# One 512-column matmul for both activation parts, in 512-column weight blocks with rows taken by fours

## The chip, the core and the metric

The kernel runs on one NeuronCore of a Trainium2 chip. The metric is the device time of one execution in microseconds (us). TensorE (PE) multiplies into PSUM, VectorE (DVE) and ScalarE (ACT) do everything elementwise, and all loads are issued in order from SyncE's queue (SP).

## The reference, cut to what matters

Two layers work on a residual stream x of 256 tokens by 2048 features, in float32. Everything is a function of x, of one conditioning vector c, and of some 580 MB of weights that are read once.

```
for layer in range(2):
    mod = silu(c) @ ada_w[layer] + ada_b[layer]          # 2048 x 12288, a matrix by ONE vector
    sh1, sc1, g1, sh2, sc2, g2 = split(mod, 6)
    h = rmsnorm(x, norm_mix) * (1 + sc1) + sh1
    proj = h @ w_in[layer]                               # 2048 x 4608: qa ka va | qb kb vb
    mixed = concat(diff_attention(...), window_gqa_sink(...)) @ w_out[layer]     # 2048 x 2048
    x = x + g1 * mixed
    h2 = rmsnorm(x, norm_mlp) * (1 + sc2) + sh2
    x = x + g2 * (square(relu(h2 @ w_up[layer])) @ w_down[layer])   # 2048 x 8192, 8192 x 2048
return rmsnorm(x, final_norm)
```

## The kernel before, in words

Activations lie with the feature on the partition: a chunk is 128 features by 256 tokens. To keep float32 accuracy on TensorE, every weight row block and every activation is split into a high part (a cast to the fp32r type) and a low part (the rest), and a product is the sum of three matmuls: weight high by activation high, weight high by activation low, weight low by activation high (`mm3`, lines 359, 360, 361; line 387 for the first row block of a product, with the same three in another order). A call of `gemm` takes a block of 1024 weight columns over all its rows of 128: per row block one DMA of 512 KB brings `raw`, `split` makes `whi` on ScalarE (line 347) and `wlo` on VectorE (line 348), and `emit` runs 8 column tiles of 128 by 3 matmuls of 256 columns into four PSUM banks (`acc`), two column tiles to a bank. Values with tokens on the partition (va, vb) go the other way round: there the weights are the moving operand, 512 columns wide, by the same three lines.

The pools set how far the engines run ahead: 6 `raw` tiles, 8 tiles for `whi` and `wlo` (four row blocks), 4 `acc` banks, 48 slots `b` of [128, 2, 256] for activations and partial sums. The order on each engine is fixed when the program is built; each engine works through its own list in order.

The product of `ada_w` by the vector is not on TensorE: VectorE multiplies and adds it row by row (`ada`, line 199), fed by its own DMAs (`araw`) into the same `raw` pool. `feed(rate)` spreads these units between the row blocks of the other products, from the start to somewhat past the start of layer 1's MLP. So VectorE has three kinds of work beside TensorE: the `wlo` of each row block, the `ada` units, and what finishes a product: `residual` (line 706) for w_out and w_down, `settle` and `fin_up` for w_in and w_up, `hilo` (lines 450, 451) for the split of a new activation.

Stages in the trace by the first load of each weight: layer 0's w_in from 26 us, w_out 314, w_up (first half of the columns, in two K groups of 8 row blocks) 465, w_down (first half of the rows) 660, w_up second half 851, w_down second half 1042; layer 1's w_in 1229, w_out 1493, w_up 1618, w_down 1809, w_up 1993, w_down 2178 to about 2388.

## Time and profile before

| what | value |
|---|---|
| device time, median of 3 runs | 2404.28 us (2403.33 to 2410.04) |
| span of the profiled execution | 2402.5 us |
| PE busy | 2293.4 us, 17875 matmuls |
| VectorE busy | 1652.5 us |
| ScalarE busy | 1165.0 us |
| read from HBM | 581.66 MB, 243 GB/s over the span |

The span runs from the first to the last instruction of the profiled execution; the timed runs are 1.8 us above it at the median, which is what lies around the span. Matmul records overlap (one lasts 284 ns and the next starts 120 ns after it), so PE's busy share says only that its queue was not empty; the distance from one start to the next says what a matmul costs in a full stream.

### The profile page before, as it was taken

What the parts mean: (1) busy time and instruction counts of PE and PEld (TensorE: products, weight loads), DVE (VectorE), ACT (ScalarE), POOL (GpSimd) and SP (SyncE); (2) the same over time, 40 slices, a digit from 0 to 9 for tenths busy, and PEclk for the clock granted to TensorE, in tenths of its full rate; (3) what the DMA queues carried; (4) which work ended last, traced back from release to release, by engine and by line L of the source; (5) the groups of instructions that cost most, each with busy time, mean ns of one, the idle gap of its engine ahead of it and who ended that gap; (6) DMA issues with size and microseconds to landing.
All of it is one profiled execution on the core that took longest, in us unless ns stands there. A gap on an engine that the chain in (4) does not pass through costs nothing.

```text
span 2402.5 us, 44175 instructions
## 1 busy us (share of the span) xinstructions
PE 2293.4 (95%) x17875; PEld 2218.0 (92%) x17875; DVE 1652.5 (69%) x1995; ACT 1165.0 (48%) x1947; POOL 0.2 (0%) x4
## 2 busy tenths in 40 slices
PE   5888999899999999999989999999999999999998
PEld 3777898899999999999989898898999999999998
DVE  6799878887876667776768887888644444454453
ACT  4445664465433334644435557645554333454343
POOL 0000000000000000000000000000000000000000
PEclk8899999999999999999999999999999999999999
DMA  8998756898677888888886994586865555555552
GB/s 285 330 316 291 235 166 210 299 328 314 202 266 275 282 272 301 299 294 296 282 273 244 309 324 133 193 281 233 302 186 184 184 185 184 181 171 194 184 183 98
DMA packets 205776, 586.66 MB, mean 244 GB/s; under 512 B 22498, under 2 KB 31364, under 8 KB 205572
## 3 DMA queue, kind: packets, MB, share of 16 engines
q1 hardware_dynamic: 205572, 583.85, 72.3%
q8 instruction: 140, 2.29, 0.4%
q14 instruction: 64, 0.52, 0.1%
HBM read 581.66 MB, written 2.10 MB: 243 GB/s over the span
## 4 chain that ended last, share of the span: by engine, by line
PE 61%; DMA 3%; DVE 2%; ACT 2%; issue 1%; SPq 0%; DVEq 0%; ACTq 0%
PE acc L360 18%; PE acc L361 18%; PE acc L359 18%; PE acc L387 3%; DMA araw<-in_ada_w_dram 2%; DVE wlo L348 1%; PE misc L586 1%; PE lg L601 1%; PE misc L495 1%; PE misc L206 0%; ACT whi L347 0%; PE lg L648 0%; PE misc L578 0%; ACT tmp L459 0%; PE misc L518 0%
## 5 line engine op out<-in xcount | busy, mean ns | idle before, releaser
L359 PE MATMUL acc<-b,whi 128*128 128x256 f32 x5000 | 1417.7, 284 | 5.8 <-ACT whi L347 5.8
L360 PE MATMUL acc<-b,whi 128*128 128x256 f32 x5000 | 1415.1, 284 | 0.0
L361 PE MATMUL acc<-b,wlo 128*128 128x256 f32 x5000 | 1409.7, 284 | 5.6 <-DVE wlo L348 5.1
L347 ACT CAST whi<-raw 128x1024 fp32r<-128x1024 f32 (+1 forms) x726 | 743.7, 1032 | 1007.3 <-PE acc L360 771.4
L348 DVE TENSOR_TENSOR wlo<-raw,whi 128x1024 fp32r<-128x1024 f32 (+1 forms) x726 | 862.9, 1200 | 451.2 <-ACT whi L347 447.8
L359 PEld LDWEIGHTS acc<-b,whi 128*128 128x128 f32 x5000 | 960.4, 192 | 10.1 <-ACT whi L347 7.2
L361 PEld LDWEIGHTS acc<-b,wlo 128*128 128x128 f32 x5000 | 955.9, 192 | 12.0 <-DVE wlo L348 8.5
L360 PEld LDWEIGHTS acc<-b,whi 128*128 128x128 f32 x5000 | 960.9, 192 | 2.8 <-issue 2.0
L199 DVE SCALAR_TENSOR_TENSOR ada<-araw,c_act,ada 128x1024 f32<-128x1024 f32 (+1 forms) x375 | 464.9, 1240 | 160.4 <-DMA araw<-in_ada_w_dram 158.2
L387 PE MATMUL acc<-b,whi 128*128 128x256 f32 x720 | 149.7, 300 | 20.2 <-ACT b L559 8.4
L387 PEld LDWEIGHTS acc<-b,whi 128*128 128x128 f32 x720 | 123.3, 205 | 24.2 <-ACT b L559 9.4
L387 PE MATMUL acc<-b,wlo 128*128 128x256 f32 x360 | 94.7, 300 | 3.5 <-DVE wlo L348 3.5
L387 PEld LDWEIGHTS acc<-b,wlo 128*128 128x128 f32 x360 | 73.7, 208 | 4.4 <-DVE wlo L348 4.4
L451 DVE TENSOR_TENSOR b<-tmp,b 128x512 fp32r<-128x512 f32 x72 | 49.5, 689 | 32.2 <-ACT b L450 31.9
L706 DVE SCALAR_TENSOR_TENSOR x<-acc,mod,x 128x256 f32<-128x256 f32 x128 | 54.8, 479 | 21.4 <-PE acc L361 21.3
L360 PE MATMUL acc<-wlo,b 128*128 128x512 f32 (+1 forms) x152 | 56.5, 372 | 3.2 <-DVE wlo L348 3.2
L208 ACT ACTIVATE misc<-misc 128x128 f32<-128x128 f32 x192 | 50.2, 261 | 18.8 <-PE misc L206 17.7
L361 PE MATMUL acc<-whi,b 128*128 128x512 f32 (+1 forms) x152 | 55.9, 367 | 0.0
L450 ACT CAST b<-tmp 128x512 fp32r<-128x512 f32 x72 | 44.6, 619 | 21.9 <-DVE tmp L797 19.4
L359 PE MATMUL acc<-whi,b 128*128 128x512 f32 (+1 forms) x152 | 52.8, 372 | 2.3 <-ACT whi L347 2.1
L559 ACT ACTIVATE b<-tmp,mod 128x256 fp32r<-128x256 f32 x62 | 34.4, 596 | 9.1 <-DVE mod L218 5.1
L360 PEld LDWEIGHTS acc<-wlo,b 128*128 128x128 f32 x152 | 28.7, 189 | 9.7 <-DVE wlo L348 5.4
(171 smaller groups left out, 1230.7 us busy)
## 6 DMA issues: line engine op xcount, KB each, us to landing
araw<-in_ada_w_dram SPq DMA_DIRECT2D x512, 256.0 KB, 4.9
raw<-in_w_up_dram SPq DMA_DIRECT2D x256, 512.0 KB, 4.6
raw<-in_w_down_dram SPq DMA_DIRECT2D x256, 512.0 KB, 4.7
raw<-in_w_in_dram SPq DMA_DIRECT2D x144, 512.0 KB, 5.5
araw<-in_ada_w_dram SPq DMA_DIRECT2D x128, 512.0 KB, 5.5
raw<-in_w_out_dram SPq DMA_DIRECT2D x64, 512.0 KB, 5.4
b<-in_x_dram SPq DMA_DIRECT2D x8, 256.0 KB, 5.0
out_dram<-tmp SPq DMA_DIRECT2D x8, 256.0 KB, 2.7
```

Of the source, the lines that this page charges most:

```text
L199: nc.vector.scalar_tensor_tensor(acc, raw[:, j, :], cc, acc, op0=ALU.mult, op1=ALU.add)
L208: nc.scalar.activation(pm[:, t * P : (t + 1) * P], pm[:, t * P : (t + 1) * P], AF.Copy, accum_out=m[:, t0 + t : t0 + t + 1])
L347: nc.scalar.copy(hi, raw)
L348: nc.vector.tensor_tensor(lo, raw, hi.bitcast(F32), op=ALU.subtract)
L359: nc.tensor.matmul(o, lhsT=lhi, rhs=rhi, start=first, stop=False, skip_group_check=True)
L360: nc.tensor.matmul(o, lhsT=lhi, rhs=rlo, start=False, stop=False, skip_group_check=True)
L361: nc.tensor.matmul(o, lhsT=llo, rhs=rhi, start=False, stop=last, skip_group_check=True)
L387: nc.tensor.matmul(banks[t // 2][:, t % 2, :], lhsT=w1[:, t * P : (t + 1) * P], rhs=a2, start=a2 is ahi and w1 is hi and t % 2 == 0, stop= ...
L450: nc.scalar.copy(hi, src)
L451: nc.vector.tensor_tensor(lo, src, hi.bitcast(F32), op=ALU.subtract)
L559: nc.scalar.activation(hi[:, j, :], t[:, j, :], AF.Identity, scale=G, bias=sh)
L706: nc.vector.scalar_tensor_tensor(x[:, j, :], bank[:, j, :], g[j], x[:, j, :], op0=ALU.mult, op1=ALU.add)
```

## The change

In layer 0 and layer 1 the products w_out, w_up and w_down, and in layer 1 also ka, qa and qb of w_in, get a new kind "s". The high and low part of an activation now lie in one slot [128, 2, 2, 256], so that weight high by both parts is one matmul of 512 columns into a whole bank, the high product in its first half and the low product in its second (line 395 of the changed kernel); weight low by activation high is a second matmul of 256 columns into the second half (line 397). A bank holds one column tile of 128, so four banks hold 512 columns: a `gemm` call of this kind takes 512 columns, one DMA brings two row blocks (still 512 KB), and `emit` runs four row blocks at a time, column tile by column tile. The halves of a bank are added when it is read: `settle` copies the first half on ScalarE and adds the second on VectorE; `residual` adds each half to x by its own instruction. ReLU and square of w_up move from two ScalarE instructions to one on VectorE. The slots `b` are twice as large and half as many. Layer 0's w_in keeps the old three matmuls, and va and kb, vb theirs. The core of the diff (comments removed by it and renamings are left out):

```diff
-KV_AT = (2, 2)
+KV_AT = (2, 3)
...
+GROUP = 4
...
-    bp = pool("bp", 48)
+    bp = pool("bp", 24)
...
-        return bp.tile([P, 2, S], dt, tag="b", name=nm("b"))
+        return bp.tile([P, 2, 2, S], dt, tag="b", name=nm("b"))
...
-        nb = width // 256
-        banks = banks or [acc_bank() for _ in range(nb)]
+        if banks is None:
+            banks = [acc_bank() for _ in range(2 if kind == "ft" else 4)]
         per = min(max(RAW // width, 1), len(rows))
         n = len(rows)
-        nf = {"f": width // P, "t": 0, "ft": 2}[kind]
+        nf = {"f": width // P, "s": 0, "t": 0, "ft": 2}[kind]
 
         def emit(chunks):
             ops = []
             for ki, hi, lo in chunks:
-                ahi, alo, aj = acts[ki]
-                a2 = (ahi[:, aj, :], None if alo is None else alo[:, aj, :])
-                ops.append((begin and ki == 0, end and ki == n - 1, hi, lo, a2))
-            if kind == "f" and len(ops) == 1 and ops[0][0] and ops[0][3] is not None:
-                _, last, hi, lo, (ahi, alo) = ops[0]
-                for w2, a2 in (((hi, lo), ahi), ((hi,), alo)):
+                act, split_, aj = acts[ki]
+                ops.append((begin and ki == 0, end and ki == n - 1, hi, lo, act, split_, aj))
+            if kind == "s":
+                for t in range(width // P):
+                    fs = slice(t * P, (t + 1) * P)
+                    bank = banks[t]
+                    for first, last, hi, lo, act, split_, aj in ops:
+                        nc.tensor.matmul(bank, lhsT=hi[:, fs], rhs=act[:, :, aj, :],
+                                         start=first, stop=False, skip_group_check=True)
+                        nc.tensor.matmul(bank[:, 1, :], lhsT=lo[:, fs], rhs=act[:, 0, aj, :],
+                                         start=False, stop=last, skip_group_check=True)
+                return
...
+            if acts[u][1]:
+                hl = split(raw.rearrange("p a b -> p (a b)"), per * width)
             for j in range(per):
-                if acts[u + j][1] is None:
+                cs = slice(j * width, (j + 1) * width)
+                if acts[u + j][1]:
+                    held.append((u + j, hl[0][:, cs], hl[1][:, cs]))
+                else:
                     held.append((u + j, raw[:, j, :], None))
-                else:
-                    held.append((u + j, *split(raw[:, j, :], width)))
-            if n - TAIL < u + per < n:
-                feed(rate)
+            if (u + per) % GROUP if kind == "s" else n - TAIL < u + per < n:
+                feed(rate * per * width / 1024)
                 continue
             emit(held)
             held = []
-            feed(rate)
+            feed(rate * per * width / 1024)
         return banks
 
-    def settle(banks, accs, last):
-        """Adds a K group's banks to the partial sums; the last group's sums are returned."""
+    def settle(banks, accs, last, kind):
+
         res = []
-        for i, b in enumerate(banks):
+        n = len(banks) // 2 if kind == "s" else len(banks)
+        for i in range(n):
             if last:
                 t = tmp()
-                if accs is None:
-                    nc.scalar.copy(t, b)
-                else:
-                    nc.vector.tensor_add(t, b, accs[i])
-                res.append(t)
-            elif accs is None:
-                a = bslot(F32)
-                nc.scalar.copy(a, b)
-                res.append(a)
+            elif accs is not None:
+                t = accs[i]
             else:
-                nc.vector.tensor_add(accs[i], b, accs[i])
-                res.append(accs[i])
+                if i % 2 == 0:
+                    pair = bslot(F32)
+                t = pair[:, i % 2]
+            if kind == "s":
+                for j in range(2):
+                    b, tj = banks[2 * i + j], t[:, j, :]
+                    if accs is not None:
+                        nc.vector.tensor_add(tj, b[:, 0, :], accs[i][:, j, :])
+                    else:
+                        nc.scalar.copy(tj, b[:, 0, :])
+                    nc.vector.tensor_add(tj, tj, b[:, 1, :])
+            elif accs is not None:
+                nc.vector.tensor_add(t, banks[i], accs[i])
+            else:
+                nc.scalar.copy(t, banks[i])
+            res.append(t)
         return res
...
-    def hilo(src, alloc):
-        hi, lo = alloc(), alloc()
-        nc.scalar.copy(hi, src)
-        nc.vector.tensor_tensor(lo, src, hi.bitcast(F32), op=ALU.subtract)
-        return hi, lo
-
-    def rope(xs, which):
+    def hilo(src):
+        hl = bslot()
+        nc.scalar.copy(hl[:, 0], src)
+        nc.vector.tensor_tensor(hl[:, 1], src, hl[:, 0].bitcast(F32), op=ALU.subtract)
+        return hl
...
-        for b, bank in enumerate(banks):
+        for b in range(len(banks) // 2):
             g = [need(l, sec, 2 * (i0 + b) + j) for j in range(2)]
             with tc.high_priority() if final else nullcontext():
                 x = X[i0 + b]
                 for j in range(2):
-                    nc.vector.scalar_tensor_tensor(
-                        x[:, j, :], bank[:, j, :], g[j], x[:, j, :], op0=ALU.mult, op1=ALU.add)
+                    for hf in range(2):
+                        nc.vector.scalar_tensor_tensor(
+                            x[:, j, :], banks[2 * b + j][:, hf, :], g[j], x[:, j, :], op0=ALU.mult, op1=ALU.add)
...
+        fkind = "f" if l == 0 else "s"
+
+        def fblocks(c0, kind, name, which):
+            w = 1024 if kind == "f" else 512
+            return [(c, w, kind, fin_rot(name, which)) for c in range(c0, c0 + 1024, w)]
+
+        blocks = (fblocks(KA, fkind, "ka", "a") + [(VA, 1024, "t", fin_va)]
+                  + fblocks(QA, fkind, "qa", "a"))
+        late = [(KB, 512, "ft", fin_kv)] + fblocks(QB, fkind, "qb", "b")
...
-            for nb in range(2):
-                banks = gemm(w_out[l], nb * 1024, 1024, rows, acts, "f", sliced["wout"])
-                residual(banks, l, 2, nb * 4, part == 1)
+            for nb in range(4):
+                banks = gemm(w_out[l], nb * 512, 512, rows, acts, "s", sliced["wout"])
+                residual(banks, l, 2, nb * 2, part == 1)
...
-            for bi, b in enumerate(banks):
-                r = tmp()
-                if accs is None:
-                    nc.scalar.activation(r, b, AF.Relu)
-                    nc.scalar.activation(r, r, AF.Square)
-                else:
-                    nc.vector.tensor_add(r, b, accs[bi])
-                    f = r.rearrange("p a b -> p (a b)")
-                    nc.vector.scalar_tensor_tensor(f, f, 0.0, f, op0=ALU.max, op1=ALU.mult)
-                u.append(hilo(r, bslot))
+            for r in settle(banks, accs, True, "s"):
+                f = r.rearrange("p a b -> p (a b)")
+                nc.vector.scalar_tensor_tensor(f, f, 0.0, f, op0=ALU.max, op1=ALU.mult)
+                u.append(hilo(r))
 
         def up(ncols, c0, groups, rate):
-            grouped_gemm(w_up[l], [(c0 + j, 1024, "f", fin_up) for j in range(0, ncols, 1024)],
+            grouped_gemm(w_up[l], [(c0 + j, 512, "s", fin_up) for j in range(0, ncols, 512)],
                          groups, get_h, rate, (l, 4))
 
         def down(k0, n, rate, final):
             acts = chunks_of(u[k0 // 2 : (k0 + n) // 2])
             rows = list(range(k0, k0 + n))
-            for nb in range(2):
-                banks = gemm(w_down[l], nb * 1024, 1024, rows, acts, "f", rate)
-                residual(banks, l, 5, nb * 4, final)
+            for nb in range(4):
+                banks = gemm(w_down[l], nb * 512, 512, rows, acts, "s", rate)
+                residual(banks, l, 5, nb * 2, final)
```

The order on TensorE shows what a column tile gets, in the first 512 or 1024 columns of the second half of layer 0's w_up (`b` the activations, `acc` the banks). Before, two column tiles of one row block:

```order
L359 MATMUL acc_9893<-b_6088,whi_10324 128x256
L360 MATMUL acc_9893<-b_6089,whi_10324 128x256
L361 MATMUL acc_9893<-b_6088,wlo_10325 128x256
L359 MATMUL acc_9894<-b_6088,whi_10324 128x256
L360 MATMUL acc_9894<-b_6089,whi_10324 128x256
L361 MATMUL acc_9894<-b_6088,wlo_10325 128x256
```

All matmuls of one `whi` and `wlo` stand together, 24 of them, and then the next row block comes. Now, the same engine at the start of a block; each pair stands twice, for the two row blocks in one `whi`:

```order
L395 MATMUL acc_8383<-b_4535,whi_8389 128x512
L397 MATMUL acc_8383<-b_4535,wlo_8390 128x256
...
L395 MATMUL acc_8383<-b_4546,whi_8400 128x512
L397 MATMUL acc_8383<-b_4546,wlo_8401 128x256
...
L395 MATMUL acc_8384<-b_4535,whi_8389 128x512
L397 MATMUL acc_8384<-b_4535,wlo_8390 128x256
```

Three matmuls became two, and both `whi` and both `wlo` of four row blocks are used in every column tile, so all four stay in use until the last of the four column tiles.

The order on VectorE at a block's end, in the second half of layer 0's w_up, before (`wlo` splits, then the low parts `b` of the four finished banks):

```order
L199 SCALAR_TENSOR_TENSOR ada_9697<-araw_10512,c_act,ada_9697 128x1024
L348 TENSOR_TENSOR wlo_10365<-raw_10362,whi_10364 128x1024
L348 TENSOR_TENSOR wlo_10455<-raw_10452,whi_10454 128x1024
L348 TENSOR_TENSOR wlo_10485<-raw_10482,whi_10484 128x1024
L451 TENSOR_TENSOR b_10424<-tmp_10420,b_10423 128x512
L451 TENSOR_TENSOR b_10431<-tmp_10427,b_10430 128x512
L451 TENSOR_TENSOR b_10438<-tmp_10434,b_10437 128x512
L348 TENSOR_TENSOR wlo_10541<-raw_10538,whi_10540 128x1024
L451 TENSOR_TENSOR b_10445<-tmp_10441,b_10444 128x512
```

Four instructions finish 1024 columns. Now, at the end of a block of 512 columns (L475 adds the second half of a bank, L844 is ReLU and square, L486 the low part):

```order
L355 TENSOR_TENSOR wlo_8837<-raw_8834,whi_8836 128x1024
L475 TENSOR_TENSOR tmp_8802<-tmp_8802,acc_8602 128x256
L475 TENSOR_TENSOR tmp_8802<-tmp_8802,acc_8603 128x256
L206 SCALAR_TENSOR_TENSOR ada_8393<-araw_8920,c_act,ada_8393 128x1024
L475 TENSOR_TENSOR tmp_8807<-tmp_8807,acc_8604 128x256
L844 SCALAR_TENSOR_TENSOR tmp_8802<-tmp_8802 128x512
L355 TENSOR_TENSOR wlo_8879<-raw_8876,whi_8878 128x1024
L475 TENSOR_TENSOR tmp_8807<-tmp_8807,acc_8605 128x256
L486 TENSOR_TENSOR b_8813<-tmp_8802,b_8813 128x512
L844 SCALAR_TENSOR_TENSOR tmp_8807<-tmp_8807 128x512
L355 TENSOR_TENSOR wlo_8885<-raw_8882,whi_8884 128x1024
L486 TENSOR_TENSOR b_8817<-tmp_8807,b_8817 128x512
```

Eight instructions finish 512 columns, and the splits of the next four row blocks, `wlo_8879` and `wlo_8885`, stand among them.

## Rows read from the trace of the kernel before

**Rows 1.** The page: span, busy time of each engine, and the chain by engine.
```profile
span 2402.5 us, 44175 instructions
PE 2293.4 (95%) x17875; PEld 2218.0 (92%) x17875; DVE 1652.5 (69%) x1995; ACT 1165.0 (48%) x1947; POOL 0.2 (0%) x4
...
PE 61%; DMA 3%; DVE 2%; ACT 2%; issue 1%; SPq 0%; DVEq 0%; ACTq 0%
```

**Rows 2.** Windows: us; busy per engine (instructions); PE clock, DMA share, GB/s.
```profile
120.00:180.00 60.00, 49.46 (x337) 43.86 (x335) 56.07 (x72) 26.21 (x58) 0.00 (x0) 0.99 0.93 318
314.00:465.00 151.00, 142.11 (x1076) 134.11 (x1075) 120.73 (x191) 75.67 (x156) 0.00 (x0) 0.99 0.67 227
465.00:565.00 100.00, 92.37 (x730) 90.18 (x729) 85.30 (x90) 53.88 (x105) 0.00 (x0) 0.95 0.93 330
565.00:660.00 95.00, 92.90 (x772) 92.43 (x771) 71.45 (x83) 51.46 (x78) 0.00 (x0) 1.00 0.69 230
...
851.00:1042.00 191.00, 189.72 (x1577) 188.91 (x1576) 135.60 (x131) 91.46 (x133) 0.00 (x0) 1.00 0.85 292
...
1300.00:1493.00 193.00, 191.40 (x1308) 172.30 (x1307) 155.18 (x213) 122.44 (x245) 0.00 (x0) 1.00 0.79 271
1493.00:1618.00 125.00, 122.65 (x941) 116.46 (x940) 104.38 (x177) 66.59 (x140) 0.00 (x0) 0.99 0.68 229
...
1809.00:1993.00 184.00, 184.00 (x1536) 184.00 (x1535) 83.61 (x76) 73.23 (x76) 0.00 (x0) 1.00 0.56 183
```

**Rows 3.** Timeline of PE, layer 1's w_down: start us, us, matmuls of 256 columns.
```profile
1849.90 0.28 PE L360 MATMUL acc<-b,whi 128*128 128x256 f32 x1
1850.02 0.28 PE L361 MATMUL acc<-b,wlo 128*128 128x256 f32 x1
...
1850.74 0.28 PE L361 MATMUL acc<-b,wlo 128*128 128x256 f32 x1
```

**Rows 4.** Timeline of PE, layer 1's va: matmuls of 512 columns.
```profile
1317.82 0.39 PE L361 MATMUL acc<-whi,b 128*128 128x512 f32 x1
1318.05 0.39 PE L359 MATMUL acc<-whi,b 128*128 128x512 f32 x1
...
1319.18 0.39 PE L361 MATMUL acc<-whi,b 128*128 128x512 f32 x1
```

**Rows 5.** Instructions by line and shape: count, busy us, mean ns, idle before.
```profile
L348 DVE TENSOR_TENSOR wlo<-raw,whi 128x1024 fp32r<-128x1024 f32 x696 | 843.1, 1223 | 447.2 <-ACT whi L347 443.8 <-ACT b L559 2.2
L347 ACT CAST whi<-raw 128x1024 fp32r<-128x1024 f32 x696 | 726.4, 1050 | 979.1 <-PE acc L360 757.7 <-DMA raw<-in_w_in_dram 90.0 <-DMA raw<-in_w_out_dram 45.9
L199 DVE SCALAR_TENSOR_TENSOR ada<-araw,c_act,ada 128x1024 f32<-128x1024 f32 x345 | 442.4, 1282 | 159.1 <-DMA araw<-in_ada_w_dram 157.5
L706 DVE SCALAR_TENSOR_TENSOR x<-acc,mod,x 128x256 f32<-128x256 f32 x128 | 54.8, 479 | 21.4 <-PE acc L361 21.3
...
L569 DVE TENSOR_TENSOR b<-tmp,b 128x512 fp32r<-128x512 f32 x28 | 19.3, 688 | 2.3 <-ACT b L559 2.3
...
L561 DVE TENSOR_SCALAR tmp<-tmp,mod 128x256 f32<-128x256 f32 x32 | 11.7, 411 | 0.0
...
L797 DVE SCALAR_TENSOR_TENSOR tmp<-tmp 128x512 f32<-128x512 f32 x16 | 10.9, 688 | 0.1
...
L795 DVE TENSOR_TENSOR tmp<-acc,b 128x512 f32<-128x512 f32 x16 | 10.6, 684 | 0.0
...
L555 DVE TENSOR_TENSOR tmp<-x,misc 128x256 f32<-128x256 f32 x8 | 3.0, 418 | 7.3 <-ACT b L538 7.3
```

**Rows 6.** Waits over the span: us in total, times, longest us.
```profile
ACT whi L347 <- PE acc L360: 771.4, 443, 4.4
...
DVE ada L199 <- DMA araw<-in_ada_w_dram: 158.2, 120, 3.6
```

**Rows 7.** Waits of VectorE from 851 to 1042 us.
```profile
DVE ada L199 <- DMA araw<-in_ada_w_dram: 28.8, 26, 2.9
```

**Rows 8.** DMA issues of the page: count, KB each, median us to landing.
```profile
araw<-in_ada_w_dram SPq DMA_DIRECT2D x512, 256.0 KB, 4.9
```

More of the change, by code (lines that the diff above doesn't have):

```diff
@@ L378, in emit, with two @@
             for ki, hi, lo in chunks:
-                ahi, alo, aj = acts[ki]
-                a2 = (ahi[:, aj, :], None if alo is None else alo[:, aj, :])
-                ops.append((begin and ki == 0, end and ki == n - 1, hi, lo, a2))
-            if kind == "f" and len(ops) == 1 and ops[0][0] and ops[0][3] is not None:
-                _, last, hi, lo, (ahi, alo) = ops[0]
-                for w2, a2 in (((hi, lo), ahi), ((hi,), alo)):
+                act, split_, aj = acts[ki]
[10 more added lines that the diff above has]
+                return
+            def two(act, split_, aj, cols):
+                if not split_:
+                    return act[:, aj, cols], None
+                return act[:, 0, aj, cols], act[:, 1, aj, cols]
+            if kind == "f" and len(ops) == 1 and ops[0][0] and ops[0][5]:
+                _, last, hi, lo, act, split_, aj = ops[0]
+                for w2, h in (((hi, lo), 0), ((hi,), 1)):
                     for t in range(nf):
@@ L387, in emit @@
                             nc.tensor.matmul(
-                                banks[t // 2][:, t % 2, :], lhsT=w1[:, t * P : (t + 1) * P], rhs=a2,
-                                start=a2 is ahi and w1 is hi and t % 2 == 0,
-                                stop=last and a2 is alo and t % 2 == 1, skip_group_check=True)
+                                banks[t // 2][:, t % 2, :], lhsT=w1[:, t * P : (t + 1) * P], rhs=act[:, h, aj, :],
+                                start=h == 0 and w1 is hi and t % 2 == 0,
+                                stop=last and h == 1 and t % 2 == 1, skip_group_check=True)
                 return
             for t in range(nf):
-                fs = slice(t * P, (t + 1) * P)
-                for first, last, hi, lo, a2 in ops:
-                    mm3(banks[t // 2][:, t % 2, :], part((hi, lo), fs), a2,
-                        first and t % 2 == 0, last and t % 2 == 1)
+                for first, last, hi, lo, act, split_, aj in ops:
+                    mm3(banks[t // 2][:, t % 2, :], part((hi, lo), slice(t * P, (t + 1) * P)),
+                        two(act, split_, aj, slice(0, S)), first and t % 2 == 0, last and t % 2 == 1)
             if kind == "f":
@@ L402, in emit @@
                     cs = slice(hf * 512, (hf + 1) * 512) if kind == "t" else slice(256, 512)
-                    for first, last, hi, lo, a2 in ops:
+                    for first, last, hi, lo, act, split_, aj in ops:
+                        a2 = two(act, split_, aj, ts)
                         if kind == "t":
-                            o = banks[tt * (width // 512) + hf].rearrange("p a b -> p (a b)")
-                            mm3(o, part(a2, ts), part((hi, lo), cs), first, last)
+                            o = banks[2 * tt + hf].rearrange("p a b -> p (a b)")
+                            mm3(o, a2, part((hi, lo), cs), first, last)
                         else:
-                            mm3(banks[1][:, tt, :], part(a2, ts), part((hi, lo), cs),
+                            mm3(banks[1][:, tt, :], a2, part((hi, lo), cs),
                                 first and tt == 0, last and tt == 1)
@@ L481, in square_sum @@
         n = NCH // 2
-        sq = tmp() if i else bslot(F32)
+        sq = tmp() if i else bslot(F32)[:, 0]
         nc.scalar.activation(sq, X[i], AF.Square)
@@ L536, in norm_x @@
         pb = spread(rstd_cols(ssq[0][:, 0, :2]) if cols is None else cols, 2)
-        r = bslot(F32)[:, 0, :]
+        r = bslot(F32)[:, 0, 0, :]
         nc.scalar.copy(r, pb[:, :S])
@@ L549, in modulated @@
         t = tmp()
-        v = bslot(F32) if whole else tmp()
-        hi, lo = (None, None) if whole else (bslot(), bslot())
+        hl = bslot(F32 if whole else F32R)
+        v = hl[:, 0] if whole else tmp()
+        hi, lo = hl[:, 0], hl[:, 1]
         for j in range(2):
@@ L595, in diff_pair @@
             es = []
-            lgs = [lgp.tile([P, 2, S], F32, tag="lg", name=nm("lg")) for m in range(2)]
+            lgs = [lg_bank() for m in range(2)]
             for qb in range(2):
@@ L667, in swa_pair @@
             av(o[:, t, :], v, g * P, wT, t == 0, t == 1)
-        return hilo(o, bslot)
+        return hilo(o)
     def chunks_of(pairs):
-        return [(hi, lo, j) for hi, lo in pairs for j in range(2)]
+        return [(hl, True, j) for hl in pairs for j in range(2)]
     def grouped_gemm(w, blocks, groups, get_act, rate, capped=None):
@@ L688, in grouped_gemm @@
                     accs[bi] = accs[bi] or [
-                        lgp.tile([P, 2, S], F32, tag="lg", name=nm("kv")) for _ in range(2)]
+                        lg_bank("kv") for _ in range(2)]
                     gemm(w, c0, width, rows, acts, kind, r, accs[bi], gi == 0, last)
```

75 lines of the change are left out of this document (43 added, 32 removed).

## The prediction

> **What bounds the kernel now.** I read the page first, then the windows stage by stage, the timeline of PE in two stages, the instructions by shape, and the waits. The page puts 61% of the chain that ended last on PE, at most 3% on anything else, and PE is busy for 95% of 2402.5 us [rows 1]. The windows show where that is the whole truth and where not. From 1809 us on PE is full to the last microsecond at the full clock, with VectorE busy for 83.61 of 184 us [rows 2]. In layer 0's w_up PE is near full too, but VectorE stands at 85.30 of 100 us and the DMAs at 0.93; in layer 1's w_out VectorE is busy for 104.38 of 125 us [rows 2]. The longest wait of all is ScalarE waiting for PE to free a `whi`, 771.4 us over the span [rows 6]: the splits run ahead of PE until the eight tiles are full. So PE sets the time, and VectorE is next in layer 0's MLP and at the end of layer 1's mixer.
>
> **What a matmul costs in a full stream.** The reader should look at start times, not at durations. Matmuls of 256 columns start at 1849.90, 1850.02 and so on to 1850.74: seven steps in 0.84 us, 0.120 us each [rows 3]. Those of 512 columns go from 1317.82 to 1319.18 in six steps, 0.2267 us each [rows 4]. The granted clock is 1.00 (2.4 GHz) in both stages, the windows from 1809 and 1300 us [rows 2]. Twice the columns cost 0.107 us more, so some 13 ns of each matmul don't depend on its columns.
>
> **The change on TensorE.** In the changed program's order 4992 column tiles get one matmul of 512 and one of 256 columns in place of three of 256. Before, 3 x 0.120 = 0.360 us; now 0.2267 + 0.120 = 0.347 us; 4992 x 0.0133 = 66 us less. The trace doesn't show a moving operand that is read in two runs of 256 with a gap between them. Its bounds: 0.213 us if the 13 ns fell away here (twice the saving; no row supports it, and I leave it out of the range), 0.240 us if it runs as two matmuls (no saving). I take 0.2267, the row with the same number of columns and the same type.
>
> The Trainium skill speaks against this (TensorE: Matmul & The Clock Gate, section "Wait — 56ns, not 53.3ns?"): a warm matmul there costs its columns plus a fixed part of about 2.5 ns. By that rule the saving would be an estimated 4992 x 2.5 ns = 12.5 us. The steps in rows 3 and 4 give 13 ns and not 2.5, so here the trace disagrees.
>
> **The change on VectorE.** A sum of 256 columns out of PSUM costs 418 ns, L555 [rows 5]; it stands for the new second-half adds. Residual instructions double, from 128 to 256: 128 x 0.479 = 61 us more. In w_up 48 tiles that ScalarE finished alone now cost VectorE two adds and ReLU-square, 2 x 0.418 + 0.688 = 1.52 us; 16 tiles with a partial sum cost four adds in place of one of 0.684 us, 0.99 us more; the first K group adds 32 x 0.418; layer 1's w_in 24 x 0.418. Sum 61 + 73 + 16 + 13 + 10 = 173 us more on VectorE, all in places I go through now. ScalarE loses about what it gains (two copies of 256 columns for ReLU and square of 512) and is busy for 48% [rows 1]; I cost it at nothing, its cover being the 979.1 us that it idles before `whi` [rows 5]. SP issues as many weight DMAs as before, of the same 512 KB.
>
> From 1809 us to the end the added work is hidden: VectorE has half of each stage free [rows 2], and the whole gain of three stages and most of the fourth comes through there, about 7 us for each stage of 512 tiles. Four places give something back. The highest VectorE share in any stretch of rows 2 is 56.07 of 60 us, 0.93; I take that as the most that it does in order.
>
> First, the first half of layer 0's w_up, 465 to 660 us. VectorE has 85.30 + 71.45 = 156.8 us of work; it gets 13.4 us (first group) and 16 x 0.99 = 15.8 us (second), 186 us. At 0.93 that takes 200 us, while PE would need 195 - 6.8 = 188 us: 12 us given back.
>
> Second, the second half of w_up, 851 to 1042 us: 135.6 + 16 x 1.52 = 160 us of work, and VectorE idles 28.8 us in front of `ada` units whose data hasn't landed [rows 7]. 189 us against PE's 191 - 6.8 = 184 us: 5 us given back. Behind such a waiting `ada` instruction stand the next `wlo` splits, and behind those PE. The two w_down stages of layer 0 get only 8 us each, and I give nothing back there.
>
> Third, layer 1's w_out: 104.38 + 32 x 0.479 = 119.7 us; at 0.93, 129 us against 125 - 3.4 = 121.6 us: 7 us. Layer 0's w_out, 120.73 + 15.3 = 136 of 151 us [rows 2], comes to 146 us, about what PE needs: nothing.
>
> Fourth, the starts of layer 1's w_in and w_up, where the sixteen `h` chunks are made while PE already uses them. A pair of row blocks costs VectorE 0.688 + 2 x 0.411 + 0.688 = 2.20 us for `h` (L561 twice, L569, and the multiply by the norm, of L569's shape) [rows 5], 1.22 us per split of 1024 columns and 1.28 us per `ada` unit. With 1024-column blocks and 0.75 units a row block that is 2.20 + 2.45 + 1.92 = 6.6 us beside 5.76 us of PE; eight pairs end 6.4 us late. With 512-column blocks it is 2.20 + 1.22 + 0.96 = 4.4 us beside 2.78 us; eight pairs end 12.8 us late, since PE passes over all of `h` in half the time. In w_up (0.6 units) the same sums give 3.4 us before and 11.3 us now. 6.4 + 7.9 = 14 us given back.
>
> **The sum.** 66 - 12 - 5 - 7 - 14 = 28 us less. The profiled execution's span goes from 2402.5 to about 2374.5 us; with the 1.8 us around it, and from the median of 2404.3 us, 2376 us.
>
> **The pools.** Eight tiles for `whi` and `wlo` held four row blocks, each freed after 2.88 us of PE, so a split had three row blocks, 8.6 us, to be ready in. Now two groups of four row blocks fill them, and a group's tiles come free at its end: the next splits have one group, 16 x 0.347 = 5.55 us, for 1.05 + 2 x 1.22 = 3.5 us of work. 2 us are left. Without `ada` that holds, so I cost it at nothing from 1809 us on. With `ada` it is the next paragraph's slower rival.
>
> **Rivals.**
> Nothing given back (0.18): VectorE's new work lies in gaps everywhere, the idle time in front of `ada` shrinks as VectorE comes later, and the full 66 us come through: 2339 us. For it: VectorE is busy for 69% only. Against it: the stages above.
>
> The queue in front of the group (0.14, slower): with 1.3 `ada` units per group VectorE and ScalarE need 3.5 + 1.7 = 5.2 of the 5.55 us, and a wait for `araw` (158.2 us in 120 waits, the longest 3.6 us [rows 6]) no longer fits behind a full pool, it stops PE. If 35% of these waits reach PE, 55 us are lost: 2431 us. It decides from about 36 us, 23% of the waits. For it: the order puts `ada` between the splits of consecutive groups. Against it: before, PE lost little in the same stages, and part of these waits is VectorE being early.
>
> The pair costs what three matmuls cost (0.06, slower): then the change doesn't do what it says on PE, and VectorE's bounds are held against unshortened stages: 200 - 195 = 5 us, 129 - 125 = 4 us, and 13 us at the two starts: 2426 us. Against it: rows 3 and 4. The rule of the skill named above would bring the time near this.
>
> The weight stream gets slower (0.10, no change): rows of 512 columns make 2 KB lines in place of 4 KB. Half the `ada` loads are such already: 512 DMAs of 256 KB on 128 partitions [rows 8]. If the stream lost a tenth where it is loaded (330 GB/s in 465 to 565 us, 292 in 851 to 1042 us [rows 2]), the first would need 11 us more and the second about 5, and as much again in the stages between: 2376 + 24 = 2400 us. The window at 120 us, full of 2 KB lines, moves 318 GB/s at a share of 0.93, that at 1809 us, 4 KB lines only, 183 GB/s at 0.56: per share the short lines are not dearer.
> The Trainium skill (Perfetto Trace Analysis, section "DMA Optimizations") says that going from 2 KB to 4 KB or 8 KB transfers can raise throughput much, which would make this rival larger; these windows don't bear it out.
>
> **How the numbers follow.** My forecast (0.52) has its own range of 2355 to 2397 us: half or one and a half times the give-backs. The range of 2340 to 2425 us reaches to the full saving on one side and into both slower rivals on the other; about 0.15 is left out. A measurement can tell 0.3%, 7 us, from no change, so faster means below 2397 us and slower above 2411 us. Faster: 0.50 + 0.18 + 0.04 = 0.72. Same: 0.02 from the forecast's end, 0.05 from the weight stream, 0.04 from the slower rivals' lower ends: 0.11. Slower: 0.17.
>
> **What would show it.** On PE: pairs that start 0.347 us after one another from 1809 us on, and three stages there of 177 us each in place of 184. On VectorE: about 1825 us busy, and a share of over 0.9 in the first half of layer 0's w_up, where PE waits for `wlo`. At the start of layer 1's w_in and w_up PE should stand waiting for `h`. The forecast is wrong if the pair costs 0.36 us, if PE waits for `whi` or `wlo` in layer 1's last three stages, or if layer 0's MLP is shorter than before by more than 20 us (nothing given back) or longer by more than 15 us (the queue).

## The result and the profile after

The changed kernel took 2374.7 us (median of 4 runs, 2370.6 to 2379.2) against 2406.7 us of the kernel before (4 runs): ratio 0.987, 95% interval 0.985 to 0.989. The forecast was 2376 us. The total is right, but two of its parts are not, and they cancel: the matmuls saved 51 us and not 66, and the stages gave back 20 us and not 38.

The page after (busy time per engine, the chain, lines with count, busy, mean ns and idle time before; the last one a DMA issue):

```profile
span 2369.8 us, 34621 instructions
PE 2245.7 (95%) x12883; PEld 1938.4 (82%) x12883; DVE 1785.0 (75%) x2356; ACT 1126.3 (48%) x1958; POOL 0.2 (0%) x4
...
PE 75%; DVE 10%; DMA 7%; ACT 4%; issue 3%; SPq 0%; DVEq 0%; ACTq 0%
...
L395 PE MATMUL acc<-b,whi 128*128 128x512 f32 x4992 | 1760.7, 397 | 23.9 <-DVE x L756 11.2
L397 PE MATMUL acc<-b,wlo 128*128 128x256 f32 x4992 | 1393.1, 283 | 9.4 <-DVE wlo L355 9.2
...
L756 DVE SCALAR_TENSOR_TENSOR x<-acc,mod,x 128x256 f32<-128x256 f32 x256 | 112.3, 479 | 15.1 <-PE acc L397 13.4
...
raw<-in_w_up_dram SPq DMA_DIRECT2D x256, 512.0 KB, 4.7
```

Against [rows 1] PE has 4992 instructions fewer and VectorE 132 us more work. What matters most to the reader is the chain that ended last: VectorE had 2% of it and now has 10%.

Windows after, of w_up (470 to 570), around the first end of a w_down block (724 to 750), of layer 1's w_out, and of a stage near the end (columns as in [rows 2]):

```profile
470.00:500.00 30.00, 18.89 (x84) 15.65 (x84) 24.96 (x35) 20.21 (x51) 0.00 (x0) 0.72 0.82 272
500.00:570.00 70.00, 66.02 (x371) 55.64 (x371) 63.36 (x76) 33.59 (x64) 0.00 (x0) 1.00 0.96 333
...
724.00:731.00 7.00, 0.97 (x9) 0.73 (x7) 6.60 (x9) 3.57 (x18) 0.00 (x0) 0.81 0.64 211
731.00:750.00 19.00, 18.74 (x96) 16.21 (x97) 10.47 (x13) 4.59 (x5) 0.00 (x0) 0.89 0.70 238
...
1500.00:1628.00 128.00, 123.60 (x712) 105.49 (x710) 118.96 (x186) 63.45 (x121) 0.00 (x0) 0.99 0.76 260
1824.00:2001.00 177.00, 177.00 (x1023) 156.07 (x1022) 89.09 (x97) 64.11 (x64) 0.00 (x0) 1.00 0.56 190
```

The last row is the clean case: the stage takes 177 us where 184 stood in [rows 2], VectorE is half idle, PE full. From 500 to 570 us VectorE is at 0.91, as foreseen, yet PE is busy for 94%. PE stands still for 11 of the 30 us before that, and for 6 of the 7 us from 724 us on.

PE at the start of that w_up (start us, us, instruction, what it waited for):

```profile
474.22 2.22 PE L529 MATMUL misc<-mean_d,tmp 128*128 128x1 f32 x16 [3.20 <-ACT tmp L517]
479.47 0.79 PE L552 MATMUL misc<-ident,n 128*128 128x128 f32 x2 [3.04 <-ACT n L545]
...
485.54 0.79 PE L395 MATMUL acc<-b,whi 128*128 128x512 f32 x1 [2.42 <-DVE b L600]
...
495.15 0.50 PE L395 MATMUL acc<-b,whi 128*128 128x512 f32 x1 [1.97 <-DVE b L604]
```

The first wait is for the squares of the last residual of w_out (0.85 us before), the third and fourth are for `h` (no such waits before). The second was there before. From 476 us, in these waits, to 489 us the granted clock is 0.50 (1.2 GHz); the window from 470 us has 0.72 in the mean.

PE at 724 us, where the first 512-column block of w_down ends:

```profile
723.81 0.28 PE L397 MATMUL acc<-b,wlo 128*128 128x256 f32 x1
723.93 1.03 PE L213 MATMUL misc<-ident,ada 128*128 128x128 f32 x8
731.26 0.77 PE L395 MATMUL acc<-b,whi 128*128 128x512 f32 x1 [6.29 <-DVE x L756]
```

VectorE in the same place:

```profile
724.40 1.23 DVE L355 TENSOR_TENSOR wlo<-raw,whi 128x1024 fp32r<-128x1024 f32 x1 [3.29 <-ACT whi L354]
725.54 0.75 DVE L204 TENSOR_SCALAR ada<-araw,c_act 128x1024 f32<-128x1024 f32 x1
726.20 1.22 DVE L355 TENSOR_TENSOR wlo<-raw,whi 128x1024 fp32r<-128x1024 f32 x1
727.33 1.28 DVE L206 SCALAR_TENSOR_TENSOR ada<-araw,c_act,ada 128x1024 f32<-128x1024 f32 x1
728.53 0.16 DVE L222 TENSOR_TENSOR mod<-mod,vecs 128x8 f32<-128x8 f32 x1
728.65 1.28 DVE L206 SCALAR_TENSOR_TENSOR ada<-araw,c_act,ada 128x1024 f32<-128x1024 f32 x1
729.85 1.26 DVE L756 SCALAR_TENSOR_TENSOR x<-acc,mod,x 128x256 f32<-128x256 f32 x3
```

PE needs a bank, the bank needs its residual (L756), that needs the gate (`mod`, L222), and the gate is written after two splits of the next weights, the first of which waited for a free `whi`. A block of 512 columns ends after half as many row blocks as one of 1024, so half as many `ada` units have been issued by then.

For the account below I took all of PE's start times, subtracted 0.2267 us per 512-column and 0.120 us per shorter matmul, and sorted what is left into steps that are 0.15 us or more too long (waits, and matmuls at half clock) and the small rest. Equal matmuls that the timeline prints as one row count as one step, and the table leaves out the first 26 us:

| stage | forecast | long steps before, after | more | small rest, more |
|---|---|---|---|---|
| layer 0, w_in and w_out | 0 | 101.8, 102.2 | 0.4 | 0.3 |
| layer 0, w_up, first half | 12 | 13.7, 22.6 | 8.9 | 0.4 |
| layer 0, w_up, second half | 5 | 1.9, 3.3 | 1.4 | 1.6 |
| layer 0, w_down, both halves | 0 | 4.4, 9.4 | 5.0 | 6.7 |
| layer 1, w_in and w_out | 13.4 | 39.1, 39.5 | 0.4 | 3.0 |
| layer 1, w_up, first half | 7.9 | 7.5, 11.3 | 3.8 | 1.1 |
| layer 1, the three last stages | 0 | 2.9, 3.1 | 0.2 | 1.1 |
| sum | 38 | 171.3, 191.4 | 20.1 | 14.2 |

66 - 20 - 14 = 32 us; the spans differ by 32.7.

### The profile page after: what moved, and what is told of

Read it like the earlier page. It is cut to its first block, busy times and chain, and to the rows that moved or that the text cites. A ratio compares the mean times of both kernels' runs of the same rounds, so it can differ in the third digit from the quotient of the medians.

```text
span 2369.8 us, 34621 instructions
## 1 busy us (share of the span) xinstructions
PE 2245.7 (95%) x12883; PEld 1938.4 (82%) x12883; DVE 1785.0 (75%) x2356; ACT 1126.3 (48%) x1958; POOL 0.2 (0%) x4
## 4 chain that ended last, share of the span: by engine, by line
PE 75%; DVE 10%; DMA 7%; ACT 4%; issue 3%; SPq 0%; DVEq 0%; ACTq 0%
PE acc L395 41%; PE acc L397 21%; DMA araw<-in_ada_w_dram 4%; DVE ada L206 3%; DVE wlo L355 3%; PE acc L368 2%; PE acc L367 2%; DMA raw<-in_w_in_dram 2%; PE acc L366 2%; PE lg L636 1%; ACT whi L354 1%; PE misc L621 1%; DVE x L756 1%; PE acc L364 1%; PE misc L529 1%
## 5 line engine op out<-in xcount | busy, mean ns | idle before, releaser
L395 PE MATMUL acc<-b,whi 128*128 128x512 f32 x4992 | 1760.7, 397 | 23.9 <-DVE x L756 11.2
L397 PE MATMUL acc<-b,wlo 128*128 128x256 f32 x4992 | 1393.1, 283 | 9.4 <-DVE wlo L355 9.2
L354 ACT CAST whi<-raw 128x1024 fp32r<-128x1024 f32 x711 | 725.1, 1049 | 903.0 <-PE acc L395 598.2
L395 PEld LDWEIGHTS acc<-b,whi 128*128 128x128 f32 x4992 | 935.6, 188 | 241.6 <-issue 18.3
L355 DVE TENSOR_TENSOR wlo<-raw,whi 128x1024 fp32r<-128x1024 f32 x711 | 851.2, 1221 | 350.0 <-ACT whi L354 345.0
L397 PEld LDWEIGHTS acc<-b,wlo 128*128 128x128 f32 x4992 | 947.1, 190 | 29.3 <-DVE wlo L355 17.3
L756 DVE SCALAR_TENSOR_TENSOR x<-acc,mod,x 128x256 f32<-128x256 f32 x256 | 112.3, 479 | 15.1 <-PE acc L397 13.4
L366 PE MATMUL acc<-b,whi 128*128 128x256 f32 x320 | 91.7, 290 | 1.5 <-ACT whi L354 1.5
L367 PE MATMUL acc<-b,whi 128*128 128x256 f32 x320 | 90.7, 287 | 0.0
L368 PE MATMUL acc<-b,wlo 128*128 128x256 f32 x320 | 89.3, 289 | 0.9 <-DVE wlo L355 0.8
L474 ACT COPY tmp<-acc 128x256 f32<-128x256 f32 x120 | 44.3, 372 | 58.2 <-PE acc L397 57.8
L475 DVE TENSOR_TENSOR tmp<-tmp,acc 128x256 f32<-128x256 f32 x152 | 61.9, 417 | 12.1 <-ACT tmp L474 11.8
L366 PEld LDWEIGHTS acc<-b,whi 128*128 128x128 f32 x320 | 62.1, 194 | 2.9 <-ACT whi L354 2.1
L368 PEld LDWEIGHTS acc<-b,wlo 128*128 128x128 f32 x320 | 60.5, 193 | 3.2 <-issue 1.7
L367 PEld LDWEIGHTS acc<-b,whi 128*128 128x128 f32 x320 | 62.0, 194 | 1.1 <-issue 1.0
L215 ACT ACTIVATE misc<-misc 128x128 f32<-128x128 f32 x192 | 50.0, 260 | 16.7 <-PE misc L213 15.0
L486 DVE TENSOR_TENSOR b<-tmp,b 128x512 fp32r<-128x512 f32 x72 | 49.1, 690 | 10.9 <-ACT b L485 9.3
```

The costliest lines, as they stand in the source:

```text
L215: nc.scalar.activation(pm[:, t * P : (t + 1) * P], pm[:, t * P : (t + 1) * P], AF.Copy, accum_out=m[:, t0 + t : t0 + t + 1])
L354: nc.scalar.copy(hi, raw)
L355: nc.vector.tensor_tensor(lo, raw, hi.bitcast(F32), op=ALU.subtract)
L366: nc.tensor.matmul(o, lhsT=lhi, rhs=rhi, start=first, stop=False, skip_group_check=True)
L367: nc.tensor.matmul(o, lhsT=lhi, rhs=rlo, start=False, stop=False, skip_group_check=True)
L368: nc.tensor.matmul(o, lhsT=llo, rhs=rhi, start=False, stop=last, skip_group_check=True)
```

## The experiments

Theory: the pair of matmuls saves 13 ns a tile, and what is given back comes from VectorE's background work (`ada`) getting later against a faster PE. Rivals: the gain comes from blocks and loads; the give-back is VectorE's new work, or the pools.

**1. The 512-column matmul written as two of 256.**

```
-   nc.tensor.matmul(bank, lhsT=hi[:, fs], rhs=act[:, :, aj, :], start=first, ...)
+   for h in range(2):
+       nc.tensor.matmul(bank[:, h, :], lhsT=hi[:, fs], rhs=act[:, h, aj, :], start=first and h == 0, ...)
```

> The changed kernel with its 512-column matmul written as two of 256 columns with the same weights; banks, blocks, groups and VectorE's work stay. Theory (the gain is 13 ns of TensorE per matmul left out, 4992 of them, and VectorE's new work costs the rest): the pair takes 0.360 us again, and the time is that of the kernel before plus VectorE's new work, 2426 us (2415 to 2438). Rival (the gain comes from the blocks of 512 columns, the two-row loads and the groups of four rows): still 2375 to 2390 us.

2429.6 us, ratio 1.010 (1.009 to 1.012). PE in a late stage:

```profile
1880.01 0.40 PE L396 MATMUL acc<-b,whi 128*128 128x256 f32 x2
1880.25 0.28 PE L398 MATMUL acc<-b,wlo 128*128 128x256 f32 x1
1880.37 0.40 PE L396 MATMUL acc<-b,whi 128*128 128x256 f32 x2
```

Three matmuls in 0.36 us again, though two of them share their weights. The whole gain hangs on the one wide matmul; blocks, groups and the new work on VectorE alone make the kernel 1% slower. The rule of 2.5 ns per matmul (the Trainium skill, TensorE: Matmul & The Clock Gate, section "Wait — 56ns, not 53.3ns?") would put this kernel an estimated 12 us behind the changed one; it was 55.

**2. The gate's units earlier.** `R1[1]`, the rate at which `ada` units are issued in the first w_down stage, 0.55 to 0.8.

```
-R1 = ([1.2, 0.2], 0.55, 0.65, 0.65)
+R1 = ([1.2, 0.2], 0.8, 0.65, 0.65)
```

> The rate of ada units in the first w_down of layer 0 goes from 0.55 to 0.8 units per load. Theory (in that stage PE stood 6.3 us before its second block because the first block's residual waited for its gate, and then ran some microseconds at half the clock): the wait and the slow stretch go, 2366 us (2362 to 2370). Rival (the stage lost its time to VectorE's amount of work): VectorE gets more ada units there, so 2375 to 2380 us.

2359.7 us, ratio 0.981 (0.979 to 0.983). PE's long steps in that stage went from 7.7 us to none; the wait of 6.29 us is gone. By the ratios it is 15 us faster than the changed kernel's first runs, more than the 8 expected. Between the two profiled executions the difference is 7.8 us (2369.8 to 2362.0 us), what the theory expected; where the rest comes from is not shown.

**3. Rows by twos.**

```
-GROUP = 4
+GROUP = 2
```

> Rows by twos: GROUP 2 in place of 4, nothing else. Theory (VectorE's total work and its due dates give the time back, not the groups): 2370 to 2376 us. Rival (groups of four rows fill the pool of whi and wlo twice only, so that every wait of VectorE reaches PE, and the starts need two more row blocks of h): waits for wlo and h fall by half and the time to 2358 to 2366 us.

2401.3 us, ratio 1.000 (0.998 to 1.001): the gain is gone, and both theories missed. PE at the end of a w_down block:

```profile
784.49 0.27 PE L397 MATMUL acc<-b,wlo 128*128 128x256 f32 x1
789.06 0.77 PE L395 MATMUL acc<-b,whi 128*128 128x512 f32 x1 [4.30 <-DVE x L756]
```

The waits of PE for the residual over the span (us in total, times, longest):

```profile
PE acc L395 <- DVE x L756: 28.9, 22, 6.0
```

VectorE there:

```profile
785.71 1.28 DVE L206 SCALAR_TENSOR_TENSOR ada<-araw,c_act,ada 128x1024 f32<-128x1024 f32 x1 [2.04 <-DMA araw<-in_ada_w_dram]
786.91 0.48 DVE L756 SCALAR_TENSOR_TENSOR x<-acc,mod,x 128x256 f32<-128x256 f32 x1
787.30 1.22 DVE L355 TENSOR_TENSOR wlo<-raw,whi 128x1024 fp32r<-128x1024 f32 x1
788.43 1.66 DVE L756 SCALAR_TENSOR_TENSOR x<-acc,mod,x 128x256 f32<-128x256 f32 x4
```

With four rows to a group the four banks of a block end over its last three quarters of 5.55 us (4.2 us); with two, over 2.1 us. The first bank is wanted back at once by the next block, and VectorE has that much less time to read it: 22 such waits, 28.9 us, where the changed kernel has 9, 11.2 us. These 17.7 us are about half of what the profiled execution lost (2369.8 to 2402.2 us); what made the other half was not taken apart. In the place shown the wait for `araw` does reach PE, the way of the slower rival in the prediction.

**4. ReLU and square back on ScalarE**, two instructions of 512 columns in place of one on VectorE.

```
-f = r.rearrange("p a b -> p (a b)")
-nc.vector.scalar_tensor_tensor(f, f, 0.0, f, op0=ALU.max, op1=ALU.mult)
+nc.scalar.activation(r, r, AF.Relu)
+nc.scalar.activation(r, r, AF.Square)
```

> ReLU and square of w_up go back to ScalarE as two instructions, 64 x 0.69 = 44 us less for VectorE, 78 us more for ScalarE. Theory (in layer 0's w_up PE waits for VectorE's amount of work): half of the 12 us that these two stages lost more than before come back, 2368 us (2364 to 2372). Rival (what PE waits for there is data and due dates, not VectorE's amount): 2373 to 2378 us.

2376.8 us, ratio 0.988 (0.987 to 0.990), no gain. PE's long steps in layer 0's two w_up stages are 23.9 us, where the changed kernel has 25.9: 2 us at most of the 6 expected. VectorE's amount of work in w_up is not what PE mainly waits for.

**5. The control.** In the changed kernel's profile a pair takes 0.3467 us from 1731 us to some 2305 us, in that of experiments 2 and 4 0.3533 us. So the changed kernel ran once more, in one set with the next three kernels.

> The changed kernel once more, on the same chip as the other runs of this set. Expected 2372 us, ratio to the kernel before 0.987 (its first interval was 0.985 to 0.989). Its first profile had the 512-column and the 256-column matmul of a pair 0.346 us apart, those of the gate, group and ReLU experiments 0.353 us in the same code. If the program decides that, this run has 0.346 again; if the chip or the moment does, it may have 0.353 and be up to 2500 pairs of the dense stages x 0.007 = 17 us longer.

2380.7 us, ratio 0.990 (0.987 to 0.992). PE of the changed kernel, first profile:

```profile
1849.92 0.39 PE L395 MATMUL acc<-b,whi 128*128 128x512 f32 x1
1850.15 0.28 PE L397 MATMUL acc<-b,wlo 128*128 128x256 f32 x1
...
1850.96 0.39 PE L395 MATMUL acc<-b,whi 128*128 128x512 f32 x1
...
1851.31 0.39 PE L395 MATMUL acc<-b,whi 128*128 128x512 f32 x1
```

The control:

```profile
1850.04 0.40 PE L395 MATMUL acc<-b,whi 128*128 128x512 f32 x1
1850.27 0.28 PE L397 MATMUL acc<-b,wlo 128*128 128x256 f32 x1
...
1851.10 0.40 PE L395 MATMUL acc<-b,whi 128*128 128x512 f32 x1
...
1851.45 0.40 PE L395 MATMUL acc<-b,whi 128*128 128x512 f32 x1
```

Four pairs in 1.39 us and in 1.41, of the same program. Between 1740 and 2280 us the mean of 1554 pairs is 0.3467 us, and of 1525 pairs 0.3533. Nearly every stretch has one of the two values and keeps it until something comes between the pairs (a wait, another kind of matmul, two of equal width in a row); the control also has a change at 1721 us, where nothing of the kind shows. The mean over the run is 0.3496 us in the first profile and 0.3515 in the control, against 0.3599 for the three matmuls before. So the program alone does not set the value. Which chip the first run was on is not known, so this pair of runs does not rule the chip out.

**6. Both kernels with `ada` nearly away from VectorE.**

```
-    acc, raw[:, j, :], cc, acc, op0=ALU.mult, op1=ALU.add)
+    acc[:, :8], raw[:, j, :8], cc, acc[:, :8], op0=ALU.mult, op1=ALU.add)
```

> The kernel before with the multiply-adds of the modulation sections on VectorE cut to 8 of their 1024 columns after the first row block; the reads of their weights stay. It leaves out most of that matrix product. It takes VectorE's background work nearly away. Theory (before, this work delays TensorE by little, since it had room there): about 2393 us, 10 us less than the kernel before. The rival, by which the change gives its time back in places that have nothing to do with this work, has no own value here; what counts is the difference to the cut of the changed kernel.

> The changed kernel with the same cut. Theory (what the change gave back, some 34 of 66 us, is the modulation work of VectorE getting later against a TensorE that is sooner: gates not ready, rows behind modulation units): the give-back goes, and this kernel is 55 to 66 us faster than the cut kernel before, about 2333 us, with no wait over 1 us for the gate at the first w_down block. Rival (the give-back is in the new blocks themselves: banks, the pools and the new operation on VectorE): the difference between the two cut kernels stays at 30 to 45 us, about 2355 us.

2382.0 us and 2347.2 us (ratios 0.990 and 0.975), 34.8 us apart, in the rival's range; uncut, in the same set, the two are 25.0 us apart. PE's long steps, here and below over the whole run, are 171.2 and 181.4 us, uncut 190.1 and 211.3 (the control). So the time that `ada` takes on VectorE accounts for about half of the give-back, and not for the rest; the loads of `ada`, its order and its due dates are still there in the cut kernels. In w_up's first half the cut leaves 11.9 before and 18.9 after, seven of the nine; no run here takes these away. And the gate's wait is still there, 4.27 us. VectorE of the cut changed kernel, then ScalarE and PE:

```profile
702.86 1.23 DVE L355 TENSOR_TENSOR wlo<-raw,whi 128x1024 fp32r<-128x1024 f32 x1 [3.18 <-ACT whi L354]
704.01 0.74 DVE L204 TENSOR_SCALAR ada<-araw,c_act 128x1024 f32<-128x1024 f32 x1
704.67 1.22 DVE L355 TENSOR_TENSOR wlo<-raw,whi 128x1024 fp32r<-128x1024 f32 x1
705.81 0.22 DVE L206 SCALAR_TENSOR_TENSOR ada<-araw,c_act,ada 128x8 f32<-128x8 f32 x1
706.07 0.17 DVE L222 TENSOR_TENSOR mod<-mod,vecs 128x8 f32<-128x8 f32 x1
...
706.29 2.04 DVE L756 SCALAR_TENSOR_TENSOR x<-acc,mod,x 128x256 f32<-128x256 f32 x5
```

```profile
701.78 1.99 ACT L354 CAST whi<-raw 128x1024 fp32r<-128x1024 f32 x2 [3.54 <-PE acc L395]
703.68 0.26 ACT L215 ACTIVATE misc<-misc 128x128 f32<-128x128 f32 x1
...
705.85 0.18 ACT L215 ACTIVATION_READ_ACCUMULATOR misc<-misc 128x1 f32 x1
```

```profile
707.70 0.76 PE L395 MATMUL acc<-b,whi 128*128 128x512 f32 x1 [4.27 <-DVE x L756]
```

The unit costs 0.22 us and the gate still comes late. On VectorE it stands in the written order behind two splits, and these behind tiles that PE frees at the end of its group. On ScalarE the eight sums that the gate is made of (L215) stand behind two casts that waited 3.54 us for the same tiles, and end at 706.03 us, 0.04 us before the gate. So taking the splits out of VectorE's way alone would not have helped here. It is the order on these engines, and VectorE's time in the units has at most the 2 us between 6.29 and 4.27.

**7. Two rates raised, twice.** `R1 = ([1.2, 0.2], 0.8, 0.65, 0.75)`, the fourth for the second w_down stage.

> The changed kernel with two of the rates by which the modulation units are spread over a stage raised: the second number of R1 from 0.55 to 0.8, as in the gate experiment, and the fourth from 0.65 to 0.75. Theory (the fourth rate does for the second w_down stage what the second did for the first: the waits of 1.2 and 0.9 us at its start for VectorE's product with the gate go): 2 to 5 us less than the gate experiment, 2355 to 2358 us, ratio 0.979 to 0.981. Rival (those waits are for the rows, not for the gate, and stay; the denser units delay the ReLU of w_up): the same as the gate experiment or up to 4 us more, 2359 to 2364 us.

> The run with the two raised rates once more. Theory (its time hung on which of the two values of a pair its last third fell into, and not on the program): a time between 2345 and 2362 us, and if its profile shows 0.3533 us a pair after 1700 us, it is some 10 us longer than before. Rival (the program sets the value): 0.3467 us there again and 2349 us within 3.

2348.8 us (0.975, 0.973 to 0.978), and in another set 2350.0 us (0.977, 0.975 to 0.979), the fastest of the kernels that leave nothing out. PE's long steps are 198.1 and 194.9 us against 200.0 of experiment 2; 2 us come from the second w_down stage (2.8 to 0.7), as expected. The other 10 us are the pairs: 0.3467 us in the last third in both runs, 0.3533 in experiment 2. The second time the rival was right: here the value came back. The two runs were on two chips, the first on that of the control, which had 0.3533 us there; so the chip alone does not set the value either. Why the same program keeps it in one case and not in another (the control) stays open.

**8. The matmuls of a group sorted by width**, four of 512 columns and then four of 256, alone and with the two rates.

```
 for first, last, hi, lo, act, split_, aj in ops:
     nc.tensor.matmul(bank, lhsT=hi[:, fs], ...)
+for first, last, hi, lo, act, split_, aj in ops:
     nc.tensor.matmul(bank[:, 1, :], lhsT=lo[:, fs], ...)
```

> The changed kernel with the matmuls of a group of four rows put in another order: the four 512-column ones of a bank first, then its four 256-column ones, instead of pairs. In the traces so far a pair takes 0.3467 us in some stretches and 0.3533 us in others of the same code, and a stretch keeps its value until PE has been disturbed; equal matmuls in a row took 0.2277 us (512 columns) and 0.1197 us (256 columns) everywhere. Theory (the second value belongs to the alternation of the two lengths, at each change from 512 to 256 columns): one change instead of four for each four pairs, 3 x 0.2277 + 3 x 0.1197 + 0.347 to 0.353, so four pairs take 1.389 to 1.396 us, 0.3473 to 0.349 each, the same in all stretches; against the control's mean of 0.3517 that is 4992 x 0.003 to 0.004 = 13 to 22 us less than its 2381, so 2359 to 2368 us. Rival (what makes the second value is something else, as memory traffic or the weights' place): the stretches keep two values, four pairs 1.387 or 1.413 us, and the time is that of the changed kernel, 2370 to 2381 us.

> The same order together with the two raised rates of the earlier run (0.8 and 0.75). Theory: the two gains add, as they are in different places: some 2345 us, 2340 to 2350, ratio 0.973 to 0.977. Rival (the rates' run owed its 2349 us to long stretches at 0.3467 us a pair, so that the order adds nothing to it): 2347 to 2356 us.

2378.3 us (0.989, 0.987 to 0.991) and 2356.1 us (0.979, 0.977 to 0.982). PE of the first:

```profile
1849.86 1.09 PE L395 MATMUL acc<-b,whi 128*128 128x512 f32 x4
1850.78 0.64 PE L398 MATMUL acc<-b,wlo 128*128 128x256 f32 x4
1851.26 1.09 PE L395 MATMUL acc<-b,whi 128*128 128x512 f32 x4
1852.19 0.63 PE L398 MATMUL acc<-b,wlo 128*128 128x256 f32 x4
...
1854.07 1.09 PE L395 MATMUL acc<-b,whi 128*128 128x512 f32 x4
```

Three groups in 4.21 us, 0.3508 us a pair, and that in all four stages from 1740 us on, in both kernels (1.40 or 1.41 us for nearly every group). With the order sorted the two values are gone, as the theory had it, but the price is their middle and not the lower one: no gain over the pairs. The first time lies in the rival's range, the second above the theory's, at the edge of the rival's.

The theory's sum failed at the equal wide matmuls. Four of them take 0.92 or 0.93 us in the rows above, where va's price gives 0.91. Over the whole trace a wide one followed by a wide one takes 0.2333 us (3545 steps), while va's in the same kernel take 0.2281 (326 steps); the last of four takes 0.2289, and the narrow ones 0.118. So a wide matmul of the new kind costs more than one of va even without a change of width, and alternation is not the whole cause. Between the changed kernel's first profile and the control, from 1740 us on, the pairs differ in the wide one alone: 0.2300 and 0.2364 us to the next start, with 0.117 for the narrow one in both. In the code va's moving operand is weights, 512 columns in one run; here it is activations, two runs of 256 with a gap. No run changes that alone, so whether it is the cause is open.

## Why the prediction was right, and where it was not

**The pair: right in kind, a quarter too large.** Experiment 1 shows that the wide matmul makes the gain. The term "3 x 0.120 = 0.360 us; now 0.2267 + 0.120 = 0.347 us" is right for the late stages of the first profile only. The row with the same number of columns was not the row for this matmul: experiment 8 has 0.2333 us where [rows 4] had 0.2267, in equal ones too. The prediction said that the trace did not show a moving operand in two runs, gave it a bound on either side (0.213 and 0.240 us), and then took the row's price as it stood. Over the run a pair took 0.3496 us, 4992 x 0.0103 = 51 us saved, in the control 42. That the forecast came within 2 us of the time is luck: the saving was 15 us too large, the give-backs 18 us.

**"I give nothing back there" was wrong** for layer 0's w_down: 5 us more in long steps (one wait for the gate alone was 6.29 us; at that place 2.18 us stood before, with the residual behind an `ada` unit that waited for its data), and about 6.7 us in the pairs' second value. The bound on VectorE's work had no place for a unit that has a due date: a block half as wide ends half as far into the list of units. Experiment 2 moves the units and the wait goes; the cut, which leaves 4.27 us of it, shows that their cost is the smaller part. That work was mis-sized as well: 173 us more were forecast for VectorE, and its busy time rose by 132.

**The first half of w_up: 12 forecast, 8.9 measured, in another place.** The step had VectorE at 0.93 of the whole stage and PE waiting for `wlo`. PE's long steps from 500 us on are 6.5 us before and 6.8 after: VectorE's 0.91 costs nothing there. Nearly all of it lies before 500 us: 7.2 before, 15.8 after, at the end of w_out's residual and at `h`. That was the fourth step's mechanism (PE passes over all of `h` in half the time), which I had put at layer 1 only, at 14 us.

**Layer 1: 21 forecast, 4 measured.** In w_up PE does wait 2.60 us for `h` (1.55 before) and the stage gives back 3.8 us, half the term. In w_in the term of 6.4 us came to 1.8 (12.2 to 14.0 us of long steps from the stage's first load to 1300 us): the sum counted 0.96 us of `ada` per `h` pair, while the order has no `ada` unit on VectorE between 1252 and 1268 us. For w_out 7 us were forecast from a share of 0.93: VectorE did reach 118.96 of 128 us, 0.93, and PE lost nothing by it. A share of 0.93 is no limit here.

**The rivals.** The pair at the price of three matmuls falls with experiment 1. The weight stream did not slow: w_up's 512 KB land in 4.7 us, the loaded window from 500 to 570 us moves 333 GB/s, all of it weights and `ada` in 2 KB lines, with 330 from 465 to 565 us before [rows 2], and the late stage 190 GB/s at a share of 0.56, with 183 at 0.56 before. The prediction's window at 120 us was no such case: by bytes it has 44% in 2 KB lines, 22% in 1 KB and 34% in 4 KB. The rule that longer lines can raise throughput (the Trainium skill, Perfetto Trace Analysis, section "DMA Optimizations") is not borne out by these windows. The queue in front of the group was not what happened, but experiment 3 shows it one step away: with groups of two, a wait for `araw` reaches PE.

## What to carry to other kernels

Merging matmuls saves what each one costs beside its columns, here 7 to 13 ns; measure it between instructions that follow one another as they will in the new order. When blocks become narrower, look at everything whose due date is counted in blocks: gates, the residual's bank, the norm behind the last block. How busy an engine is over a stage foretold none of this; what stood in front of which instruction in the queue at the end and at the start of a stage did. Two numbers in the order took 13 to 16 us of PE's long steps away (211.3 us in the control, 198.1 and 194.9 in experiment 7), nearly half of the 32.7 us by which the spans before and after differ.

## What was not expected of the hardware

In the same code 512- and 256-column matmuls in turn take 0.3467 or 0.3533 us a pair, over hundreds of microseconds at a granted clock of 1.00. Between the changed kernel's two profiles the difference lies in the wide one, 0.2300 or 0.2364 us, where va's wide ones, one after the other, take 0.2277 us. The same program had 0.3467 us from 1731 us on in one profile and 0.3533 from 1728 us on in another, some 10 us of its time. What chooses it is open; sorted by width it is 0.3508 us throughout, with 0.2333 for a wide one followed by a wide one.
